# Start addresses modulo 256 of the split-weight rings and the gated sums in a differential-attention and retention trunk

## The chip, the cores and the metric

The kernel runs on one core of a Trainium2 chip. The metric is the time of one execution on the device in microseconds (us), as the median of several runs.

## The reference

Two inputs of 512 rows by 1024 columns (`x_prompt` and `x_sample`) go through the same two layers and a final RMS norm. All is fp32.

```python
for i in range(DEPTH):                       # DEPTH = 2
    h = rms_norm(x, norm_g[i], NORM_EPS)
    if i % 2 == 0:  x = x + diff_attention(h, da_w_in, ..., da_w_out, lambda_init)
    else:           x = x + bidir_retention(h, ret_w_in, ..., ret_w_out)
return rms_norm(x, final_norm_g, NORM_EPS)
```

Differential attention: `proj = h @ w_in` gives q and k (16 heads of 128, with rotary embedding), v and a gate (2048 each). For each of 8 heads two softmaxes are subtracted, `a = p0 - lam * p1`, and `o = a @ v` (256 columns). `o` is RMS-normed, multiplied by `silu(gate)`, and multiplied by `w_out`.

Bidirectional retention: `proj = h @ w_in` gives q and k (8 heads of 128, rotated), v and a gate (2048 each). For each head a forward and a backward sum over the rows with decaying weights are added; the sum is normed, gated and multiplied by `w_out` in the same way.

## The kernel before

**Split operands.** Every large product works on fp32r operands that are split into a high and a low part, and runs three passes (`PASSES`: high by high, high by low, low by high). Each matmul instruction multiplies a stationary operand of 128 by 128, which is loaded into TensorE beforehand, with a moving operand of 512 or 256 columns, and adds to a PSUM bank.

**Projections.** Each layer's input projection is done with a Strassen-like scheme of seven products over the two inputs and two halves of the weights. `make_b` makes the seven split activations (`B11` ... `T4`, four tiles each, high and low in one tile). A `Unit` handles 256 or 512 columns of the weights: `prep` loads, combines and splits weights into tiles of the ring `ws`; `product` multiplies. In a "pair" unit the weights are stationary and 512 columns of an activation move (the matmul at L599); in a "wide" unit, for v, the activation is stationary and 256 columns of weights move (L609). Results go through ACT, DVE and DRAM to the next stage.

**Attention.** For each head, input and block of 128 rows: `scores` (L1116, stationary q, moving k of 512 columns), exponentials on ACT, the difference, transposes (L1161) and `av` (L1181, stationary v, moving `aT` of 256 columns). `weigh` multiplies by the gate and splits the result into `oT` (two tiles, high and low), and `out_step` multiplies it by the output weights (L891: stationary `oT`, moving a `ws` tile of 512 columns) and adds to the rows `x` with the norm's factor. **Retention** has `state2` (L1339), `score2` (L1315) and `av2` (L1359 with stationary v and moving `aT` of 256 columns, L1367), and the same `weigh` and `out_step`.

**Order.** Every operation is entered in a `Plan` with a guessed cost and the buffers that it reads and writes. The plan simulates the engines and issues the instructions in the order that it finds. It knows buffers, not addresses.

**Where the tiles lie.** SBUF is given out by pools in this order: `sm` (small columns, each taking 32 bytes), `cp` (activations that are not in the arena, tables), `ar` (the arena), `wk` (all rings of work tiles: `ws` of 7, `raw`, `st`, `c`, `e`, `m`, `os`). The arena is one tile, cut by hand:

```python
arena = ar.tile([P, 18 * 1024 + 80], F32R, tag="arena", name="arena")
lo = 32 + at * 1024 + shift                  # in floats; slot number at, shift 0, 16 or 32
```

`ssf` holds sums of squares for the input and final norms: twelve columns of one float, each a tile of its own in `sm` (L917, L924, L1017).

In the built program the starts within a partition are these. Sizes of tiles and steps inside them are multiples of 256 bytes, so each start modulo 256 holds for all slices that the matmuls read.

| what | byte | modulo 256 |
|---|---|---|
| `cp` tiles, activations among them | 2,848 and on | 32 |
| arena | 52,896 | 160 |
| slots with shift 0: activations; attention's q, `aT`; retention's v | | 32 |
| slots with shift 16: attention's k, v; retention's q, `aT`, `kt` | | 96 |
| slots with shift 32: `oT`; retention's k | | 160 |
| `wk`: `ws` and all other rings | 126,944 and on | 224 |

Of the kernel before, what the change touches and what calls it, by code (L numbers as in the profile page):

```python
# [9 lines left out]
F32 = mybir.dt.float32  # L10
F32R = mybir.dt.float32r
# [4 lines left out]
P = 128  # L16
S = 512
# [236 lines left out]
def trunk_kernel(  # L254
# [12 lines left out]
    sm = ctx.enter_context(tc.tile_pool(name="sm", bufs=1))  # L267
    cp = ctx.enter_context(tc.tile_pool(name="cp", bufs=1))
    ar = ctx.enter_context(tc.tile_pool(name="ar", bufs=1))
# [7 lines left out]
    places = {}  # L277
    cnt = [0]

    def view(pool, tag, i, size, shape, dt=F32):  # L280


        if size % 16 and pool in (cp, wk):
            pool = sm
        if (tag, i) not in places:
            places[tag, i] = pool.tile([P, size], F32, tag=f"{tag}{i}", name=f"{tag}_{i}", bufs=1)
        n = math.prod(shape[1:])
        t = places[tag, i][0:shape[0], 0:n]
        if dt != F32:
            t = t.bitcast(dt)  # L290
        if len(shape) == 3:
            t = t.rearrange("p (a b) -> p a b", a=shape[1])
        elif len(shape) == 4:
            t = t.rearrange("p (a b c) -> p a b c", a=shape[1], b=shape[2])
        return t

    def work(tag, shape, bufs, dt=F32, name=None):
        size = SIZE.get(tag, shape[1])
        return Buf(plan, tag, bufs, lambda i: view(wk, tag, i, size, shape, dt))

    arena = ar.tile([P, 18 * 1024 + 80], F32R, tag="arena", name="arena")

    def slot(n, shape, dt=F32R, shift=0):

        size = math.prod(shape[1:])
        at = None if n in (12, 13) or n >= 20 else n if n < 12 else n - 2
        if at is None:
            assert not shift  # L310
            cnt[0] += 1
            label = f"b_{cnt[0]}"
            return Buf(plan, f"b{n}", 1, lambda i: cp.tile(shape, dt, tag=f"b{n}", name=label))
        assert dt == F32R
        lo = 32 + at * 1024 + shift

        def make(i):
            t = arena[:, lo:lo + size]
            return t.rearrange("p (a b) -> p a b", a=shape[1]) if len(shape) == 3 else t
        b = Buf(plan, f"b{n}", 1, make)  # L320
        b.also = Buf(plan, f"edge{at + 1 if shift else at}", 1, None)
        return b

    def const(shape, tag, dt=F32, size=None):
        return Buf(plan, tag, 1, lambda i: view(cp, tag, i, size or math.prod(shape[1:]), shape, dt))
# [27 lines left out]
    def bank(tag, name=None):  # L353
        return Buf(plan, tag, BUFS[tag], lambda i: view(pj if tag == "pj" else sc, tag, i, S, [P, S]))
# [469 lines left out]
        return rr  # L824

    def new_oT(g):
        return [slot(16 + 2 * g + a, [P, 2, S], F32R, 32) for a in range(2)]

    def load_qk(src, i, shift):
        t = slot(i, [P, 2, S], F32R, shift)  # L830
# [339 lines left out]
    def av(i):  # L1170

        h, g, t = tiles[i]
        aT, v = st[i]['aT'], vt[h, g]
        o = bank("o")

        def fn():
            n = 0
            for e in range(2):
                for a, b in PASSES:
                    for j in range(NT):  # L1180
                        nc.tensor.matmul(o[:, e * 256:(e + 1) * 256], v[b][:, j, e * P:(e + 1) * P], aT[a][:, j, :],  # L1181
                                         start=(n == 0), stop=(n % 12 == 11), skip_group_check=True)
                        n += 1
        pe(2.76, fn, [*aT, *v], [o])
        if t == 0:
            settle(h - 1, g)
            oT[h, g] = new_oT(g)
        st[i].update(o=o, sq=weigh(o, sg[h, g], oT[h, g], t // 2, GUARD))
# [160 lines left out]
    def av2(b, c):  # L1349
# [29 lines left out]
        if c == 0:  # L1379
            settle(h - 1, g)  # L1380
            oT[h, g] = new_oT(g)
# [152 lines left out]
```

## Time and profile before

| | |
|---|---|
| median of 3 runs | 1808.67 us (1808.62 to 1810.62) |
| profiled execution, span | 1807.0 us from its first to its last instruction |
| profiled execution, own time | not given apart from its span; the runs' median is 1.67 us above the span |
| TensorE matmuls, weight loads | busy 99% and 86% of the span, 10,299 each |
| VectorE (DVE), ScalarE (ACT), GpSimd (POOL) | busy 82%, 50%, 9% |
| granted TensorE clock | 0.999 |

How to read it: the profile lists groups of instructions by line and tiles, with their busy time, the mean duration of one in ns, and the idle time before them. Matmuls are pipelined and their ends are modelled: a matmul of 512 columns is shown with about 390 ns although the next one starts about 230 ns after it. The time from one start to the next is read from stretches of many matmuls. PE stands for the matmuls, PEld for the weight loads, which run beside matmuls.

### The profile page before, as it was taken

To read this page: it belongs to the slowest core of one execution; us is meant where nothing else is said; L and a number is where in the kernel's file an instruction comes from. 1 tells how busy PE (TensorE), PEld (TensorE's weight loads), DVE (VectorE), ACT (ScalarE), POOL (GpSimd) and SP (SyncE) were. 2 spreads that over 40 slices of the span, in tenths; PEclk is the share of its full clock that TensorE was granted. 3 is DMA by queue.
4 is the path that set the end of the run, shared out by engine and by line. 5 is a ranking of instruction groups with operands and counts; after the bars stand their busy time and mean duration, and the time that the engine had idled before them with its cause. 6 is when DMAs were issued, how large, how long until landed. Compare 5 with 4: busy or idle time off the path is not lost.

```text
span 1807.0 us, 27780 instructions
## 1 busy us (share of the span) xinstructions
PE 1794.9 (99%) x10299; PEld 1558.1 (86%) x10299; DVE 1477.1 (82%) x2319; ACT 895.1 (50%) x1856; POOL 169.5 (9%) x323
## 2 busy tenths in 40 slices
PE   9999999999999999999999999999999999999998
PEld 6789889898988888888888888898989898888887
DVE  7958787778699888888888897787887967888887
ACT  7753444433434565554555866444434355444346
POOL 1000000000000022222322300000000000111113
PEclk9999999999999999999999999999999999999999
DMA  6444455555545685444554524464657559765662
GB/s 217 134 126 137 161 140 178 184 168 155 174 126 175 201 334 198 178 156 159 190 204 140 190 73 146 140 210 146 205 156 228 151 170 396 272 238 182 225 218 94
DMA packets 162767, 328.81 MB, mean 182 GB/s; under 512 B 12724, under 2 KB 76872, under 8 KB 162632
## 3 DMA queue, kind: packets, MB, share of 16 engines
q1 hardware_dynamic: 162304, 326.71, 54.1%
q8 instruction: 81, 1.33, 0.3%
q14 instruction: 54, 0.44, 0.1%
q10 hardware_dynamic: 328, 0.34, 0.1%
HBM read 209.55 MB, written 117.44 MB: 181 GB/s over the span
## 4 chain that ended last, share of the span: by engine, by line
PE 93%; DVE 2%; DMA 2%; ACT 2%; issue 1%; POOL 0%; SPq 0%; POOLq 0%; DVEq 0%; ACTq 0%
PE pj L599 20%; PE pj L891 19%; PE sc L599 10%; PE pj L609 10%; PE o L599 8%; PE o L1181 5%; PE sc L1116 5%; PE sc L609 5%; PE o L609 2%; PE o L1359 2%; PE tp L1161 2%; PE sc L1315 1%; PE o L1367 1%; PE tp L1339 1%; DMA raw<-in_ret_w_out_dram 1%
## 5 line engine op out<-in xcount | busy, mean ns | idle before, releaser
L891 PE MATMUL pj<-ws,arena 128*128 128x512 f32 x1542 | 391.2, 397 | 0.0
L891 PEld LDWEIGHTS pj<-ws,arena 128*128 128x128 f32 x1542 | 277.7, 188 | 52.7
L599 PE MATMUL pj<-b,ws 128*128 128x512 f32 x1080 | 265.0, 392 | 0.0
L599 PEld LDWEIGHTS pj<-b,ws 128*128 128x128 f32 x1080 | 201.4, 188 | 43.0
L403 DVE TENSOR_TENSOR ws<-st,ws 128x512 fp32r<-128x512 f32 (+1 forms) x192 | 147.9, 774 | 74.8 <-ACT ws L400 56.7
L896 DVE SCALAR_TENSOR_TENSOR b<-pj,crr,b 128x512 f32<-128x512 f32 (+1 forms) x257 | 189.9, 744 | 21.4 <-PE pj L891 21.0
L403 DVE TENSOR_TENSOR ws<-raw,ws 128x512 fp32r<-128x512 f32 (+1 forms) x164 | 141.5, 868 | 71.3 <-ACT ws L400 61.0
L400 ACT CAST ws<-st 128x512 fp32r<-128x512 f32 (+1 forms) x192 | 132.4, 693 | 121.4 <-PE pj L599 36.4
L599 PE MATMUL sc<-arena,ws 128*128 128x512 f32 x768 | 186.8, 392 | 0.0
L599 PE MATMUL o<-arena,ws 128*128 128x512 f32 x744 | 180.0, 393 | 1.1 <-ACT m L385 0.6
L599 PEld LDWEIGHTS sc<-arena,ws 128*128 128x128 f32 x768 | 144.0, 188 | 31.3
L400 ACT CAST ws<-raw 128x512 fp32r<-128x512 f32 (+1 forms) x164 | 125.7, 772 | 87.0 <-PE o L599 45.0
L599 PEld LDWEIGHTS o<-arena,ws 128*128 128x128 f32 x744 | 138.4, 188 | 31.7 <-DVE arena L463 1.4
L599 PE MATMUL pj<-arena,ws 128*128 128x512 f32 x648 | 160.3, 392 | 0.4 <-DVE arena L463 0.4
L599 PEld LDWEIGHTS pj<-arena,ws 128*128 128x128 f32 x648 | 120.8, 188 | 26.7 <-DVE arena L463 0.7
L1134 ACT ACTIVATE b<-sc,nm 128x512 f32<-128x512 f32 x128 | 88.0, 689 | 66.9 <-DVE nm L1124 66.5
L636 ACT COPY c<-pj 128x512 f32<-128x512 f32 x104 | 60.9, 586 | 119.7 <-PE pj L599 66.4
L609 PE MATMUL pj<-ws,b 128*128 128x256 f32 x960 | 116.8, 276 | 0.0
L609 PEld LDWEIGHTS pj<-ws,b 128*128 128x128 f32 x960 | 113.2, 188 | 0.7
L1116 PE MATMUL sc<-arena 128*128 128x512 f32 x384 | 101.2, 395 | 0.3 <-ACT b L1134 0.3
L1181 PEld LDWEIGHTS o<-arena 128*128 128x128 f32 x768 | 93.1, 188 | 2.7
L1181 PE MATMUL o<-arena 128*128 128x256 f32 x768 | 93.7, 278 | 0.0
(207 smaller groups left out, 2855.9 us busy)
## 6 DMA issues: line engine op xcount, KB each, us to landing
qk<-os SPq DMA_DIRECT2D x192, 256.0 KB, 3.6
arena<-qk SPq DMA_DIRECT2D x96, 512.0 KB, 5.8
raw<-in_da_w_in_dram SPq DMA_DIRECT2D x64, 512.0 KB, 5.1
v<-os SPq DMA_DIRECT2D x64, 512.0 KB, 4.3
arena<-v SPq DMA_DIRECT2D x64, 512.0 KB, 4.1
raw<-in_ret_w_in_dram SPq DMA_DIRECT2D x48, 512.0 KB, 4.8
os<-g SPq DMA_DIRECT2D x32, 512.0 KB, 7.4
g<-e SPq DMA_DIRECT2D x48, 256.0 KB, 4.6
```

The costliest lines, as they stand in the source:

```text
L400: act(n, lambda: nc.scalar.copy(dst(), src()), r, w)
L403: dve(n, lambda: nc.vector.tensor_tensor(dst(), src(), hi().bitcast(F32), op=ALU.subtract), r, w)
L599: nc.tensor.matmul(ps.t, a[u][0]()[:, k, :], bt[k][:, v, :], start=(opens and k == 0 and i == 0), stop=(k == 3 and i == 2), skip_group_che ...
L609: nc.tensor.matmul(ps[:, (t % 2) * 256:(t % 2) * 256 + 256], bt[k][:, v, t * P:(t + 1) * P], a[u][0]()[:, k, :], start=(opens and t % 2 == ...
L636: act(S, lambda c=c, ps=ps: nc.scalar.copy(c.t, ps.t), [ps], [c])
L891: nc.tensor.matmul(ps[:, here], o[a][:, e, t * P:(t + 1) * P], u[b][:, e, here], start=(m == 0), stop=(m == 5))
L896: axpy(n, lambda half=half, here=here, ps=ps: nc.vector.scalar_tensor_tensor(half, ps[:, here], rr[:, t % 2:t % 2 + 1], half, op0=ALU.mult ...
L1116: nc.tensor.matmul(s.t, q[:, a, t * P:(t + 1) * P], k[:, b, :], start=(n == 0), stop=(n == 2))
L1134: act(840, lambda j=j, s=s, m=m: nc.scalar.activation(p[:, j, :], s.t, AF.Exp, bias=m.t, accum_out=sm[:, 2 * j + n:2 * j + n + 1]), [s, m] ...
L1161: nc.tensor.transpose(tp[:, j * P:(j + 1) * P], p[:, 0, j * P:(j + 1) * P], ident.t)
L1181: nc.tensor.matmul(o[:, e * 256:(e + 1) * 256], v[b][:, j, e * P:(e + 1) * P], aT[a][:, j, :], start=(n == 0), stop=(n % 12 == 11), skip_g ...
L1359: nc.tensor.matmul(o[:, e * 256:(e + 1) * 256], v_[v][:, 2 * c + j, e * P:(e + 1) * P], a_[:, u, j * 256:(j + 1) * 256], start=(e == 0 and ...
```

## The change

The arena grows by 16 floats (64 bytes). The twelve tiles of `ssf` become columns of one tile of 32 floats (128 bytes instead of 12 x 32 = 384), which moves everything behind them down by 256 bytes and leaves it where it was modulo 256. `wk` begins 192 bytes lower: `ws` and all other work rings start at 32 modulo 256 instead of 224. `oT` gets shift 64 instead of 32 floats, so it starts at 32 modulo 256 instead of 160. Activations, attention's q, k, v and `aT`, and retention's q, k, v, `kt` and `aT` keep their starts modulo 256. Instructions, their number and their order stay.

```diff
         if size % 16 and pool in (cp, wk):
             pool = sm
+            if tag == "ssf":
+                if tag not in places:
+                    places[tag] = sm.tile([P, 16 + 16], F32, tag=tag, name=tag, bufs=1)
+                return places[tag][:, i:i + 1]
...
-    arena = ar.tile([P, 18 * 1024 + 80], F32R, tag="arena", name="arena")
+    arena = ar.tile([P, 18 * 1024 + 96], F32R, tag="arena", name="arena")
...
     def new_oT(g):
-        return [slot(16 + 2 * g + a, [P, 2, S], F32R, 32) for a in range(2)]
+        return [slot(16 + 2 * g + a, [P, 2, S], F32R, 64) for a in range(2)]
```

## The prediction

> **What bounds the kernel now.** I read the page's busy times and chain first, then the groups by line, then the chain in order of time and the timeline at single matmuls.
>
> ```profile
> PE 1794.9 (99%) x10299; PEld 1558.1 (86%) x10299; DVE 1477.1 (82%) x2319; ACT 895.1 (50%) x1856; POOL 169.5 (9%) x323
> PE 93%; DVE 2%; DMA 2%; ACT 2%; issue 1%; POOL 0%; SPq 0%; POOLq 0%; DVEq 0%; ACTq 0%
> ```
>
> TensorE carries 93% of the chain. A busy PE is not a PE at its peak, so the question is how far apart matmuls start ("spacing"). The chain in order of time gives it for unbroken stretches (start, length, what):
>
> ```profile
> 169.04 5.44 PE sc L609 x48
> 210.01 8.24 PE pj L599 x36
> 853.26 2.83 PE o L1181 x24
> 1783.58 13.76 PE pj L891 x60
> ```
>
> A 512-wide matmul follows the last after 8.24/36 = 228.9 ns in L599 and 13.76/60 = 229.3 ns in L891; a 256-wide one after 113.3 ns in L609 and, in this stretch of L1181, after 117.9. Nothing is waited for inside these stretches, and still the spacing isn't one number. Here is what it can depend on: a weight load runs beside the matmul before its own. The timeline shows it where the moving tile changes from `b` to `arena`:
>
> ```profile
> 212.36 1.79 PEld L599 LDWEIGHTS pj<-arena,ws 128*128 128x128 f32 x8
> 212.59 1.76 PE L599 MATMUL pj<-arena,ws 128*128 128x512 f32 x7
> ```
>
> The first load of the new tile starts at 212.36, its matmul at 212.59, one spacing later. So while one matmul streams its moving rows from SBUF, the stationary rows of the next are read from SBUF too. The change alters where these two streams start relative to each other. I call "distance" the start of the moving operand minus that of the stationary one, modulo 256 bytes. From the addresses given above: L599 moves operands at 32 past weights at 224, distance 64. L891 moves weights at 224 past `oT` at 160, distance 64. L609 moves weights at 224 past operands at 32, distance 192. After the change all three have distance 0.
>
> These are the groups concerned (count, busy us, mean ns of one), and L1359, which is 256 wide like L609 but has distance 64 (moving `aT` at 96, stationary `v` at 32):
>
> ```profile
> L891 PE MATMUL pj<-ws,arena 128*128 128x512 f32 x1530 | 389.8, 398 | 0.0
> L599 PE MATMUL pj<-b,ws 128*128 128x512 f32 x1080 | 265.0, 392 | 0.0
> L599 PE MATMUL sc<-arena,ws 128*128 128x512 f32 x768 | 186.8, 392 | 0.0
> L599 PE MATMUL o<-arena,ws 128*128 128x512 f32 x744 | 180.0, 393 | 1.1 <-ACT m L385 0.6 <-DVE arena L463 0.3
> L599 PE MATMUL pj<-arena,ws 128*128 128x512 f32 x648 | 160.3, 392 | 0.4 <-DVE arena L463 0.4
> L609 PE MATMUL pj<-ws,b 128*128 128x256 f32 x960 | 116.8, 276 | 0.0
> L609 PE MATMUL sc<-ws,arena 128*128 128x256 f32 x768 | 89.6, 276 | 0.0
> L609 PE MATMUL pj<-ws,arena 128*128 128x256 f32 x576 | 73.1, 277 | 0.0
> L609 PE MATMUL o<-ws,arena 128*128 128x256 f32 x384 | 45.0, 277 | 0.0
> L599 PE MATMUL sc<-b,ws 128*128 128x512 f32 x120 | 29.1, 391 | 0.0
> L1359 PE MATMUL o<-arena 128*128 128x256 f32 x384 | 48.9, 276 | 0.0
> ```
>
> L599 has 1080 + 768 + 744 + 648 + 120 = 3,360 matmuls; with L891's 1,530 that is 4,890 of 512 columns. L609 has 960 + 768 + 576 + 384 = 2,688 of 256.
>
> **Part 1: the 512-wide matmuls.** Three successive matmuls of L599 near 210.5 us, one row each, from the groups in a window that holds that one alone:
>
> ```profile
> L599 PE MATMUL pj<-b,ws 128*128 128x512 f32 x1 | 0.4, 388 | 0.0
> L599 PE MATMUL pj<-b,ws 128*128 128x512 f32 x1 | 0.4, 392 | 0.0
> L599 PE MATMUL pj<-b,ws 128*128 128x512 f32 x1 | 0.4, 394 | 0.0
> ```
>
> The durations repeat in this cycle of three: A (388), B (392), C (394). Their mean is 391.3 and the mean spacing of the same stretch 228.9, so I read a spacing as the row's duration less 162.4. The cycle doesn't follow the buffers (in L891 it runs at other places of the six), so it is a matter of timing between the two streams. How they stand at distance 0 the trace shows at a few places only: the last matmul of a group overlaps the first weight load of the next line. The last of L599 before L609 has moving 32 and, beside it, a load from 32: distance 0. So has the last of L891 before L599 (224 and 224). One after A, that is in place B (1170.2 us), one in place C (1178.8), one in place A (1032.1):
>
> ```profile
> L599 PE MATMUL pj<-b,ws 128*128 128x512 f32 x1 | 0.4, 397 | 0.0
> L599 PE MATMUL pj<-b,ws 128*128 128x512 f32 x1 | 0.4, 393 | 0.0
> L891 PE MATMUL pj<-ws,arena 128*128 128x512 f32 x1 | 0.4, 389 | 0.0
> ```
>
> Their mean is 393.0, 1.7 ns over the cycle's: one step costs little on average, though place B pays 5. It also throws the next ones off. The three matmuls behind the event at 1032.1 us, behind one of kind C at 626.2 and behind one of kind B at 638.4 (L599 into L1116, 32 and 32):
>
> ```profile
> L599 PE MATMUL pj<-arena,ws 128*128 128x512 f32 x3 | 0.9, 396 | 0.0
> L1116 PE MATMUL sc<-arena 128*128 128x512 f32 x3 | 0.9, 395 | 0.0
> L1116 PE MATMUL sc<-arena 128*128 128x512 f32 x3 | 0.9, 393 | 0.0
> ```
>
> Their mean is 394.7, 3.4 ns over. No run of matmuls at distance 0 exists in this trace; the two bounds nearest to it are +1.7 (the step itself) and +3.4 (what follows it). After the change each matmul is both, and I take +3.0, nearer the followers. Sum: 4,890 x 3.0 ns = 14.7 us, all on the path, since inside these stretches the chain holds nothing but PE. The farther bounds are A for good, 388, which is -3.3 ns or -16.1 us, and the slowest steady row of a 512-wide stretch (L1116 near 856.7 us, distance 64), 398, which is +6.7 ns or +32.8 us:
>
> ```profile
> L1116 PE MATMUL sc<-arena 128*128 128x512 f32 x2 | 0.6, 398 | 0.0
> ```
>
> The Trainium skill, page "TensorE: Matmul & The Clock Gate", section "Step-by-step: what each phase is for", speaks against any cost: it says that TensorE reads SBUF through two independent ports, one for the streamed operand and one for the weights. By that rule this term would be 0. The 388 to 398 of one shape with nothing waited for show that something more is at work here, whether or not it is the distance.
>
> **Part 2: the 256-wide matmuls.** L609 at distance 192 and L1359 at distance 64 both stand at 276, the 113.3 ns spacing. A step at distance 0 (the last of L1181, moving 32, before L1116's load from 32, at 1002.5 us) gives
>
> ```profile
> L1181 PE MATMUL o<-arena 128*128 128x256 f32 x1 | 0.3, 277 | 0.0
> ```
>
> one ns more. I take 0 for the 2,688. The other end is L1181's 117.9 ns, +4.6 each or +12.4 us; a gain below 113.3 no row shows.
>
> **Part 3: the other rings.** All of `wk` moves from 224 to 32, so `raw`, `st`, `c`, `e`, `m` and `os` do as well. A DVE operation on tiles at 224 and one whose SBUF tiles are in the arena at 32, and the same for ACT:
>
> ```profile
> L403 DVE TENSOR_TENSOR ws<-st,ws 128x512 fp32r<-128x512 f32 x160 | 108.9, 685 | 56.7 <-ACT ws L400 56.2
> L403 DVE TENSOR_TENSOR arena<-tp,arena 128x512 fp32r<-128x512 f32 x64 | 43.8, 685 | 4.9 <-ACT arena L400 4.4
> L400 ACT CAST os<-m 128x512 fp32r<-128x512 f32 x64 | 38.5, 621 | 34.3 <-DVE m L701 33.3 <-DMA qk<-os 0.9
> L400 ACT CAST b<-m 128x512 fp32r<-128x512 f32 x8 | 4.6, 619 | 0.0
> ```
>
> 685 and 685, 621 and 619: the start makes no difference there, and PE's 99% hides a nanosecond or two in either. Transfers are the same in number, size and order; I cost them at nothing, hidden by the buffers that PE works ahead of, and the chain's 2% of DMA (36 us) is what they could touch if they did change.
>
> **Part 4: `ssf` as one tile.** No instruction is added, and the plan orders by buffers, not addresses. If neighbouring columns made one engine wait for another, this row pair shows the place:
>
> ```profile
> L924 POOL TENSOR_TENSOR rsf<-ssf,mhalf x16: 537/554/1304, 1007.1 to 1801.9; 128x1 f32<-128x1 f32 x16
> POOL rsf L924 <- ACT ssf L917: 22.5, 12, 6.5
> ```
>
> Sixteen powers of about 0.55 us on a POOL that is busy 9% of the span; each is needed a norm later. Only the last, at 1801.9, has no cover: below 0.6 us. I take 0.
>
> **Sum.** On the profiled execution, 1807.0 + 14.7 = 1821.7 us of span. The runs' median of 1808.67 lies 1.67 above that span, so 1823.4.
>
> **Rivals.** *Much slower* (0.18): at distance 0 the streams lock in the worst way seen, 398 at 512 columns and 117.9 ns at 256. For it: both are steady states of this trace, and L1181 stays in its one for 24 matmuls. Against it: single steps at distance 0 gave 389, 393 and 277. Price: 32.8 + 12.4 = 45.2 us, 1853.9.
>
> *No difference* (0.13): timing alone makes the cycle, and a constant distance only shifts where it begins. For it: distance 64 and 192 give the same 276, and L1181 shows both 113.3 and 117.9 at one distance. Against it: in place B the same step costs 392 at distance 64 and 397 at 0. Price 0, 1808.7. The skill's two ports, above, would make this the outcome.
>
> *Faster* (0.19): distance 0 keeps the load of the next weights in step with the streaming operand, so that they never want the same rows and every matmul is an A. For it: place A at distance 0 cost 389, hardly over 388, and a 256-wide matmul at 0 is as cheap as any. It decides if the step after an A is an A again. Against it: the step behind 1032.1's 389 was among three that mean 396. Price: -3.3 x 4,890 = -16.1 us, 1792.6.
>
> That the change doesn't do what it says I exclude: 384 bytes less 128 leaves 256, so all before the arena keeps its place modulo 256, and 64 bytes more of arena put `wk` at 32.
>
> **Numbers.** My forecast (0.50) is slower by 8 to 17 us for the bounds 1.7 and 3.4, so 1816 to 1826 of its own. Measurement tells about 0.2%, 3.6 us, from no change. Faster 0.19, same 0.13, slower 0.50 + 0.18 = 0.68. The range has to reach into the two outer rivals: 1797 to 1846 leaves out the last third or so of each of their ways, some 0.15 together.
>
> **What would show it.** Right: L599's stretch of 36 takes about 8.35 us instead of 8.24, its rows mean 394 to 395, L609's stay at 276, and DVE and ACT keep their durations. Wrong: L599 at 388 (faster), at 391 to 392 (no difference), or at 398 with L609 at 281 (much slower). If the time moves while these rows don't, the cause is not the distance but a wait, which the chain would name outside PE.

## The result and the profile after

The changed kernel takes 1823.58 us (median of 4 runs, 1822.9 to 1823.79) against 1808.77 before (1808.62 to 1810.62): a ratio of 1.008, 95% interval 1.0066 to 1.0094. The forecast was 1823.4. The time is the forecast one; the way to it is not. Some executions, of the kernel before too, show a mean granted clock of 0.998 instead of 0.999 and take about 1.8 us more; the text says where a profile is of such an execution. Lines behind 284 stand 4 further down after the change: L599 is L603, L609 is L613, L891 is L895, L1359 is L1363, L1367 is L1371.

The page after, first part and chain:

```profile
span 1821.8 us, 27780 instructions
PE 1808.3 (99%) x10299; PEld 1577.3 (87%) x10299; DVE 1477.6 (81%) x2319; ACT 895.5 (49%) x1856; POOL 169.9 (9%) x323
PE 93%; DVE 2%; DMA 2%; ACT 2%; issue 1%; POOL 0%; SPq 0%; POOLq 0%; DVEq 0%; ACTq 0%
```

TensorE's busy time grew by 13.4 us and that of its weight loads by 19.2; DVE and ACT stayed within 0.5. The chain has the same shares. They are whole percents, 18 us each, and can't exclude a wait alone; but span less TensorE's busy time is 13.5 us after 12.1, so waits grew by 1.4 us net at most. Now the chain in order of time (start, length, what):

```profile
168.91 5.76 PE sc L613 x48
211.36 8.16 PE pj L603 x36
```

The same stretches took 5.44 and 8.24 us before. That is, the 256-wide matmuls of the projections went from 113.3 to 120.0 ns apart, the 512-wide ones from 228.9 to 226.7: one of the two slower, the other faster. The groups by line of the changed kernel (count, busy us, mean ns of one):

```profile
L895 PE MATMUL pj<-ws,arena 128*128 128x512 f32 x1530 | 389.5, 398 | 0.0
L603 PE MATMUL pj<-b,ws 128*128 128x512 f32 x1080 | 263.1, 390 | 0.0
L603 PE MATMUL sc<-arena,ws 128*128 128x512 f32 x768 | 185.2, 390 | 0.0
L603 PE MATMUL o<-arena,ws 128*128 128x512 f32 x744 | 178.8, 391 | 1.1 <-ACT m L389 0.6 <-DVE arena L467 0.3
L603 PE MATMUL pj<-arena,ws 128*128 128x512 f32 x648 | 159.2, 390 | 0.7 <-ACT arena L473 0.4 <-DVE arena L467 0.3
L613 PE MATMUL pj<-ws,b 128*128 128x256 f32 x960 | 123.0, 283 | 0.0
L613 PE MATMUL sc<-ws,arena 128*128 128x256 f32 x768 | 94.8, 283 | 0.0
L613 PE MATMUL pj<-ws,arena 128*128 128x256 f32 x576 | 76.6, 284 | 0.0
L1363 PE MATMUL o<-arena 128*128 128x256 f32 x384 | 50.4, 280 | 0.0
L613 PE MATMUL o<-ws,arena 128*128 128x256 f32 x384 | 47.3, 283 | 0.0
L603 PE MATMUL sc<-b,ws 128*128 128x512 f32 x120 | 28.8, 389 | 0.0
```

L613 sums to 341.7 us, 17.2 more than before. L603 sums to 815.1, 6.1 less. L895 is 0.3 less. L1363, whose own operands kept their starts, is 1.5 more. These four give +12.3 of the 14.8 us. L1116, L1181, L1339 and L1367, short groups of attention and retention that kept their starts too, are 2.5 more together. Idle time adds 1.4 us, and smaller groups give as much back.

### The profile page after: what moved, and what is told of

Same layout as the page of the kernel before. It is cut to its first block, busy times and chain, and to the rows that moved or that the text cites. A ratio compares the mean times of both kernels' runs of the same rounds, so it can differ in the third digit from the quotient of the medians.

```text
span 1821.8 us, 27780 instructions
## 1 busy us (share of the span) xinstructions
PE 1808.3 (99%) x10299; PEld 1577.3 (87%) x10299; DVE 1477.6 (81%) x2319; ACT 895.5 (49%) x1856; POOL 169.9 (9%) x323
## 4 chain that ended last, share of the span: by engine, by line
PE 93%; DVE 2%; DMA 2%; ACT 2%; issue 1%; POOL 0%; SPq 0%; POOLq 0%; DVEq 0%; ACTq 0%
PE pj L603 20%; PE pj L895 18%; PE sc L603 10%; PE pj L613 10%; PE o L603 8%; PE sc L613 5%; PE o L1185 5%; PE sc L1120 5%; PE o L613 3%; PE o L1363 2%; PE tp L1165 2%; PE o L1371 1%; PE tp L1343 1%; PE sc L1319 1%; DMA raw<-in_ret_w_out_dram 1%; DMA raw<-in_da_w_in_dram 1%
## 5 line engine op out<-in xcount | busy, mean ns | idle before, releaser
L895 PE MATMUL pj<-ws,arena 128*128 128x512 f32 x1542 | 390.9, 397 | 0.0
L895 PEld LDWEIGHTS pj<-ws,arena 128*128 128x128 f32 x1542 | 277.6, 188 | 52.8
L603 PE MATMUL pj<-b,ws 128*128 128x512 f32 x1080 | 263.1, 390 | 0.0
L603 PEld LDWEIGHTS pj<-b,ws 128*128 128x128 f32 x1080 | 201.4, 188 | 41.2
L603 PE MATMUL sc<-arena,ws 128*128 128x512 f32 x768 | 185.2, 390 | 0.0
L603 PE MATMUL o<-arena,ws 128*128 128x512 f32 x744 | 178.8, 391 | 1.1 <-ACT m L389 0.6
L603 PEld LDWEIGHTS sc<-arena,ws 128*128 128x128 f32 x768 | 143.9, 188 | 29.8
L603 PEld LDWEIGHTS o<-arena,ws 128*128 128x128 f32 x744 | 138.4, 188 | 30.6 <-DVE arena L467 1.4
L603 PE MATMUL pj<-arena,ws 128*128 128x512 f32 x648 | 159.2, 390 | 0.7 <-ACT arena L473 0.4
L603 PEld LDWEIGHTS pj<-arena,ws 128*128 128x128 f32 x648 | 120.9, 188 | 25.9 <-DVE arena L467 0.6
L613 PE MATMUL pj<-ws,b 128*128 128x256 f32 x960 | 123.0, 283 | 0.0
L613 PEld LDWEIGHTS pj<-ws,b 128*128 128x128 f32 x960 | 119.1, 192 | 0.6
L613 PE MATMUL sc<-ws,arena 128*128 128x256 f32 x768 | 94.8, 283 | 0.0
```

The costliest lines, as they stand in the source:

```text
L603: nc.tensor.matmul(ps.t, a[u][0]()[:, k, :], bt[k][:, v, :], start=(opens and k == 0 and i == 0), stop=(k == 3 and i == 2), skip_group_che ...
L613: nc.tensor.matmul(ps[:, (t % 2) * 256:(t % 2) * 256 + 256], bt[k][:, v, t * P:(t + 1) * P], a[u][0]()[:, k, :], start=(opens and t % 2 == ...
L895: nc.tensor.matmul(ps[:, here], o[a][:, e, t * P:(t + 1) * P], u[b][:, e, here], start=(m == 0), stop=(m == 5))
```

## The experiments

**Theories.** D: the distance between the streaming operand's start and that of the operand being loaded, modulo 256 bytes, sets the spacing of a long run. Rivals: the gated sums carry the loss (O); a wait through the other rings or the `ssf` tile (W); the absolute start of a stream (A).

**One ring at a time, and the starts split by kind of unit.** Four kernels, beside 1808.69 us for the kernel before. The first is the changed kernel with `oT` back at 160:

```diff
-        return [slot(16 + 2 * g + a, [P, 2, S], F32R, 64) for a in range(2)]
+        return [slot(16 + 2 * g + a, [P, 2, S], F32R, 32) for a in range(2)]
```

> The ring of split weights at 32 as in the changed kernel, the gated sums oT back at 160. Theory D (the distance between the streaming and the loaded operand sets the spacing in a long run): L599 and L609 stand as in the changed kernel, 226.7 and 120 ns, which is -6 and +17 us against before; only L891 (distance now 128) and the lines that start behind it can differ: 1820 us, within 3. Rival O (the gated sums carry the loss): 1809. Rival W (a wait from the other rings or the ssf tile, which are here as in the changed kernel): 1823 to 1824, with the added time outside L609.

The second leaves `oT` at 32 and puts `wk` back to 224:

```diff
-    arena = ar.tile([P, 18 * 1024 + 96], F32R, tag="arena", name="arena")
+    arena = ar.tile([P, 18 * 1024 + 144], F32R, tag="arena", name="arena")
```

> The gated sums oT at 32 and ssf as one tile as in the changed kernel, the ring of split weights and all other work rings back at 224. Theory D: L599 and L609 as before the change, 229 and 113.3 ns; L891 at distance 192 and the short groups behind it may move by a few us: 1807 to 1812. Rival O: 1823. Rival W for the ssf tile alone: above 1809 with a longer wait on POOL in the norm of the rows.

The third has both arena and `oT` so that all starts are as before the change, and then shifts the weights of pair units alone:

```diff
+        if tag == "ws" and "ws" not in places:
+            places["ws"] = wk.tile([P, 6 * 1088 + 1040], F32, tag="ws", name="ws", bufs=1)
+        if tag == "ws":
+            lo = 1088 * i + (16 if len(shape) == 4 else 0)
+            t = places["ws"][:, lo:lo + math.prod(shape[1:])].bitcast(dt)
...
-        return work("e", [P, S], 8, name=name)
+        return work("e", [P, S], 7, name=name)
```

> Weights of pair units (stationary in L599) start at 32 and weights of wide units (moving in L609) and of the output product (moving in L891) at 224, by an offset inside the ring's places; oT at 160; one buffer less in ring e, to make room. Theory D: L599 has distance 0 and 226.7 ns, L609 distance 192 and 113.3 ns, L891 as before: 1808.8 - 6 = 1803 us, within 2, plus what the missing e buffer costs (see the run of that alone). Rival O or W (distance is not the cause): 1809 or more.

The fourth is the third without the shift:

> Starts as before the change, all distances as before, ssf as one tile, and one buffer less in ring e: the comparison for the run with split starts. If neither the ssf tile nor the eighth buffer of e matters: 1808.8, within 1. If one of them matters: above 1810, with waits on e or ssf in the chain.

Measured, in this order: 1825.65 us (ratio 1.0095, 1.008 to 1.011), 1815.36 (1.0033, 1.0021 to 1.0044), 1813.55 (1.0026, 1.0016 to 1.0036), 1808.9 (0.9999, 0.999 to 1.0009).

The last settles W for two of its places: `ssf` as one tile and one `e` buffer less cost nothing, so the third can be read against it. In the first, L603 and L613 stand as in the changed kernel (but for 1.4 us in one L603 group, since its profile has a clock of 0.998): the weights' ring alone makes the +17 and the -6. Its time is 2.7 us above D's range all the same. L891, now at distance 128, takes 3.0 us more than before, and L1359 and L1367 take 2.1 more:

```profile
L895 PE MATMUL pj<-ws,arena 128*128 128x512 f32 x1530 | 392.8, 400 | 0.0
```

O in its pure form is out, but the second run is 3 us above what D gave it. About half of that is clock: four of its six executions, the profiled one among them, have 0.998 (0.73 from 25 to 31 us of the span, where the kernel before has 1.00), and the two others took 1813.42 and 1813.8 us. Its groups:

```profile
L895 PE MATMUL pj<-ws,arena 128*128 128x512 f32 x1530 | 393.2, 400 | 0.0
L603 PE MATMUL pj<-b,ws 128*128 128x512 f32 x1080 | 264.9, 392 | 0.0
L613 PE MATMUL sc<-ws,arena 128*128 128x256 f32 x768 | 89.6, 276 | 0.0
L1363 PE MATMUL o<-arena 128*128 128x256 f32 x384 | 50.2, 279 | 0.0
L1371 PE MATMUL o<-arena,b 128*128 128x256 f32 x192 | 27.7, 279 | 0.0
```

L603 and L613 are as before, but for 1.5 us more in the L603 group that runs at the lower clock. L895, of which only the stationary operand moved (distance 64 to 192), has +3.4 us: where the loaded operand lies does slow the streaming one. And L1363 and L1371 have +1.3 and +0.7 although nothing of theirs moved. They run directly or soon behind L895. Before, L1367 (now L1371) had:

```profile
L1367 PE MATMUL o<-arena,b 128*128 128x256 f32 x192 | 27.0, 276 | 0.0
```

The longest stretch of L891, 13.76 us before, gives the spacing at the other three distances: 0 (changed kernel), 128 (first run) and 192 (second run).

```profile
1798.53 13.63 PE pj L895 x60
1802.00 13.97 PE pj L895 x60
1790.00 14.02 PE pj L895 x60
```

That is 227.2, 232.8 and 233.7 ns after 229.3: here too the distance orders the spacings.

The third run missed. The chain of it:

```profile
74.59 8.16 PE pj L611 x36
167.94 5.65 PE sc L621 x48
1172.81 4.10 PE pj L621 x36
```

The 512-wide matmuls are at 226.7 as expected (L599 is L611 here), but the 256-wide ones (L621) hold 117.7 ns at the same distance of 192 at which they hold 113.3 in the kernel before. So D in its simple form falls: one distance, two spacings. This run alone shows both: in each of retention's four wide units an early stretch of 36 has 113.9 ns (third line), and all longer ones have 117.7. What differs from the kernel before is the runs before L621, now at 226.7, and the places of the ring, which are the same modulo 256 but lie elsewhere (in one tile, 1,088 floats apart). From here on theory E: a run has more than one steady spacing, and the entry decides which.

**Other distances, and all starts shifted together.** Four kernels beside 1808.92 us. In the first two only the offset of wide units' weights in the split ring changes, with base and arena so that pair units stay at 32 and the output product at 224. The first has 16 here, the second 32 in its place:

```diff
-            lo = 1088 * i + (16 if len(shape) == 4 else 0)
+            lo = 1088 * i + (0 if len(shape) == 4 else 16 if shape[1] == 4 else 48)
```

> As the first run with split starts (pair units' weights at 32, the output product's at 224, oT at 160, one e buffer less), but the wide units' weights at 96, so L609 has distance 64 instead of 192. Theory E (a run of 256-wide matmuls has more than one steady spacing; which one it falls into depends on distance and on how it is entered): either 113.3 ns, which gives 1803 us, or 117.8, which gives 1813.5; L1359, which had distance 64 before, stood at 113.3 more often than not, so 113.3 is a little likelier. Theory D in its simple form (each distance has one spacing) says 113.3 and 1803, since 64 gave 113.3 in L1359.

> As the run before, but the wide units' weights at 160, so L609 has distance 128. Only single steps of 128 were seen: they cost 117 to 118 ns where the other matmuls around stood at 113. Theories D and E both expect 117.8 or more: 1813 to 1820 us.

The third is the kernel before with `arena` 16 floats larger than in the changed one and `ssf` as one tile:

> All work rings at 96, oT at 160: L599 has distance 192, L609 64, L891 192. Theory D: L599 not at 226.7; single steps of 192 cost 2 to 7 ns more than those of 64 in the same place, so 230 to 233 ns, +3 to +13 us; L609 113.3 to 117.8, 0 to +12 us; L891 as in the run with oT alone moved, +3. Together 1813 to 1835. If distance were without effect: 1809.

The fourth is the kernel before with `ssf` as one tile and a pad of 32 bytes in front. It keeps every distance and moves all by 32 bytes:

```diff
+    pad = sm.tile([P, 8], F32, tag="pad", name="pad", bufs=1)
     ident = const([P, P], "ident")
```

> Every tile of SBUF used by TensorE starts 32 bytes later than before the change (activations at 64, weights at 0, oT at 192, k at 128), all distances as before; ssf as one tile. Theories D and E: the distances decide alone, so 1808.8, within 2, with 228.9 and 113.3 ns. Rival A (the absolute start of a stream decides, for instance against lines of 64 bytes): L599 and L609 leave these spacings, down to 213 and 107 if a stream that starts on a line has one line less to read, which would be about 5% less time.

Measured, in this order: 1814.82 us (1.0033, 1.002 to 1.0046), 1820.5 (1.0063, 1.0048 to 1.0078), 1839.8 (1.017, 1.0153 to 1.0187), 1809.1 (1.0001, 0.9992 to 1.0011). The third missed its range by 4.8 us: L603 takes 14.1 us more where 13 was the upper end, L613 11.2 more, and L1363 and L1371 2.1 more, which the estimate hadn't. The chains of the third (first three lines) and of the fourth:

```profile
75.64 8.40 PE pj L603 x36
171.39 5.65 PE sc L613 x48
1814.56 14.02 PE pj L895 x60
```

```profile
75.20 8.24 PE pj L604 x36
168.97 5.44 PE sc L614 x48
```

Shifted together, the spacings are those of before to the last digit: rival A falls for a shift of 32 bytes. It falls for 128 bytes as well: L895 has distance 192 here with its operands at 96 and 160, and in the run with `oT` alone moved with 224 and 32, and its long stretch takes 14.02 us in both. At distance 192 the 512-wide matmuls take 8.40/36 = 233.3 ns, the worst of the four distances. L621 at distance 64 stood at 117.7 in the first of these runs, at 128 at 120.0 in the second (5.65 and 5.76 us for 48). So 64 gave the slower of E's two values, not the likelier one and not that of D.

**Is it the entry?** The split kernel again (distance 192 in the wide units), where the first matmul of P1, P2 and P4 of each wide unit is cut into narrower ones over the same columns, another cut in each of the eight units. The sums are the same; the two streams are shifted once against each other.

```diff
+    KICKS = [{(0, 0): [0, 128, 256]}, {(0, 0): [0, 64, 256]}, {(0, 0): [0, 192, 256]},
+             {(0, 0): [0, 128, 256], (0, 1): [0, 128, 256]}, {(0, 0): [0, 32, 256]}, {(0, 0): [0, 96, 256]},
+             {(0, 0): [0, 64, 128, 192, 256]}, {(0, 0): [0, 160, 256]}]
...
+                        cuts = KICKS[self.nth_wide].get((k, i), [0, 256]) if t == 0 and op in KICK_OPS else [0, 256]
+                        for c0, c1 in zip(cuts, cuts[1:]):
```

> The split starts with L609 at distance 192, and in each of the eight wide units the first matmul of P1, P2 and P4 is cut into pieces of another width (128+128, 64+192, 192+64, two matmuls of 128+128, 32+224, 96+160, 4x64, 160+96 in turn), which shifts the streams against each other once at the entry of a run. Theory E (two steady spacings at distance 192, chosen at the entry): some cuts send the rest of the run to 113.3 ns, others leave it at 117.8; with all of them at 113.3 the time would be 1805, with none 1816. Rival D2 (with L599 at distance 0 something that lasts makes L609 slower, not its entry): all runs stay at 117.8, 1814 to 1816.

One run: 1814.4 us beside 1808.64 (at a clock of 0.998, which accounts for about 1.8 us of it). The chain in order of time; one stretch of each of the eight units in turn:

```profile
169.84 5.44 PE sc L633 x48
303.92 5.65 PE sc L633 x48
381.55 5.44 PE sc L633 x48
458.71 5.65 PE sc L633 x48
1186.39 5.44 PE sc L633 x48
1284.28 5.65 PE sc L633 x48
1364.30 5.44 PE sc L633 x48
1443.37 5.65 PE sc L633 x48
```

Two values and nothing between: 113.3 ns behind the cuts 128+128, 192+64, 32+224 and 4x64, 117.7 behind the others. The stretches shown lie behind further matmuls of the same unbroken run, so what one cut matmul sets at the entry holds. A cut can also make a run slower: the stretches of 36, at 113.9 ns without cuts, take 4.24 and 4.25 us, 117.9 ns, behind the cuts 96+160 and 160+96. That is E, and D2 falls. Each cut was tried in one unit only, and fast and slow units alternate; but without cuts, and with one cut for all (next), the long runs of all eight units stand alike, so the units themselves don't explain it.

**The best of it, and the same cuts at distance 0.** The cut 128+128 in all units of the split kernel, and the eight cuts in the changed kernel itself, beside 1808.67 us:

> Split starts as in the first run with them, and the first matmul of P1, P2 and P4 of every wide unit cut into 128+128. Theory E: L599 at 226.7 ns, -5 us; L609 at 113.3 ns in all long runs; each of about 28 cuts costs about 0.12 us, +3 us. Together 1806 us, 2 to 3 below the kernel before. If the cut only works in the one unit in which it was tried: 1814.

> The changed kernel itself (all distances 0) with the eight cuts at the entries of L609, one kind for each wide unit. Theory E1 (at distance 0 only one steady spacing exists): all runs of L609 return to 120 ns, whatever the cut, 1824 to 1827 us. Theory E2 (at distance 0 too there is a faster one that is only never entered): some units at 113.3, each of them worth 2 us.

Measured: 1805.2 us (ratio 0.9981, 0.9972 to 0.9989) and 1827.12 (1.0102, 1.0086 to 1.0117). The groups of the first, the chain of the second:

```profile
L618 PE MATMUL pj<-b,ws 128*128 128x512 f32 x1080 | 263.0, 390 | 0.0
L631 PE MATMUL sc<-ws,arena 128*128 128x256 f32 x768 | 89.6, 276 | 0.0
```

```profile
132.17 8.16 PE pj L612 x36
168.83 5.76 PE sc L625 x48
```

The first has both fast spacings and beats the kernel before by 3.5 us (2 to 5 by the interval) and the changed one by 18. The rings behind `ws` (`st`, `c`, `os`, most of `e` and `m`) lie at 32 in it as in the changed kernel, so W has no ground there either. In the second no cut changes the spacing: L625 is back at 120.0 everywhere, E1, and the cuts only add 3.5 us to the changed kernel's time. At distance 0 no other steady spacing was reached by any of the eight cuts.

**The fourth distance.** All rings and `oT` at 160 (`arena` at 128 instead of 96 floats, `oT` shift 32), one run:

> All work rings at 160, oT at 160: L599 and L609 have distance 128, L891 distance 0. It completes the four distances in steps of 64. L609 at 120 ns as in the run with the wide units' weights at 160, +17 us; L599 between 226.7 and 233.4 ns, the ends seen at 0 and 192, -7 to +15 us; L891 as in the changed kernel, 0: 1818 to 1841. If the spacing at 512 columns rose step by step with the distance (226.7, 229, ..., 233.4) it would be 231, and the time 1833.

1837.54 us beside 1808.76. The chain:

```profile
75.41 8.36 PE pj L603 x36
170.97 5.76 PE sc L613 x48
302.98 5.69 PE o L613 x48
1812.41 13.64 PE pj L895 x60
```

It shows 232.2 ns at 512 columns, inside the range given. L613 stands at 120.0 in the first wide unit, and in the long runs of the seven others at about 118.6 (third line): two spacings at this distance too. L895, at distance 0 with both operands at 160, is where it was with both at 32. All distances in steps of 64 bytes:

| distance | 512 columns, ns apart | 256 columns, ns apart |
|---|---|---|
| 0 | 226.7 | 120.0 |
| 64 | 228.9 | 117.7 |
| 128 | 232.2 | 120.0 or 118.6 |
| 192 | 233.3 | 113.3 or 117.7, by the entry |

The table is of the projections' long runs. L1359's shorter ones at distance 64 stood near 113.3 in the kernel before (276 ns in the row), so 64 has more than one spacing as well.

## Why the prediction was right, and where not

**Right in time, wrong in both terms.** It had 14.7 us on the 512-wide matmuls and 0 on the 256-wide ones. The groups show -6.4 (L599 and L891) and +17.2. That the sums agree is chance: two errors of 21 and 17 us cancel, helped by some 4 us in other groups and idle time that the sum didn't hold.

**The step that failed in part 1** is the reading of "+1.7 and +3.4" as bounds for a long run. They were single steps of distance 0 in the midst of others, and what followed them was at distance 64 again, a disturbed cycle. Two of the three rows behind the +3.4 are of L1116 besides, compared with L599's cycle, and L1116's own mean before is 395:

```profile
L1116 PE MATMUL sc<-arena 128*128 128x512 f32 x384 | 101.2, 395 | 0.3 <-ACT b L1134 0.3
```

Left to itself, distance 0 has no cycle: L603 settles at one value, 226.7 ns, 2.2 below the old mean. The rival *Faster* described just this, "every matmul is an A" (A 226, its bound 388 against the 389 and 390 measured), and for the 4,890 it had the direction, with 6.4 us instead of 16.1: L891 is broken up, mostly into runs of 6 and 12, and gained 0.3 us in all.

**The step that failed in part 2** is "I take 0", from one L1181 matmul of 277 ns. The changed kernel shows why one step misleads. Two rows of it, the first matmul of L613 behind L603, at 163.0 us, and the two next:

```profile
L613 PE MATMUL o<-ws,arena 128*128 128x256 f32 x1 | 0.3, 277 | 0.0
L613 PE MATMUL o<-ws,arena 128*128 128x256 f32 x2 | 0.4, 283 | 0.0
```

The first step of a run at distance 0 is as cheap as ever; the next is not, and the run stays at 120.0 ns to its end. The upper end that I gave, 117.9, was too low as well: long runs pay 6.7 ns each, and the groups 17.2 us instead of 12.4.

**The rivals.** *Much slower* had the lock and the place of it (L609) right, and 512 columns wrong. *No difference* is refuted for this kernel: in the run with `oT` alone moved, only the stationary operand of L891 lies elsewhere, and its streaming matmuls take 393.2 us instead of 389.8. The Trainium skill, page "TensorE: Matmul & The Clock Gate", section "Step-by-step: what each phase is for", states two independent read ports. This run doesn't agree with a cost of 0 drawn from that: whatever the ports are, the two reads are not independent in time.

**Parts 3 and 4 held.** The rows of the changed kernel that answer to those of before:

```profile
L407 DVE TENSOR_TENSOR ws<-st,ws 128x512 fp32r<-128x512 f32 x160 | 109.0, 686 | 55.3 <-ACT ws L404 55.0
L404 ACT CAST b<-m 128x512 fp32r<-128x512 f32 x8 | 4.6, 619 | 0.0
POOL rsf L928 <- ACT ssf L921: 22.5, 12, 6.4
```

686 after 685, 619 after 619, and the wait on `ssf` is 22.5 us in all as before.

**A term that was missing:** lines that moved nothing. L1359 and L1367 pay +1.5 and +0.7 us, and nearly the same in the run where only `oT` moved. The runs together tie this to L891, behind which they start: L1359 takes 48.8 to 48.9 us in every kernel in which L891 has distance 64, the split ones too, and 50.2 to 50.4 in every one in which it has another. No run changed the entry of these lines by itself, so that they keep the spacing with which they are entered stays likely, not shown.

**Open.** What in SBUF or TensorE makes the two reads meet, and why some cuts of the entry lead to the faster spacing and others don't. Distances between the steps of 64 bytes were not run.

## What to carry to other kernels

Where TensorE is the bound, read matmul spacing from stretches of the chain, not from busy shares, and look whether the same shape has several; if so, the relative start of streaming and stationary tiles is a thing to set, for each shape by itself (here 0 for 512 columns, 192 for 256). A steady run can't be priced from single steps: equal matmuls can settle at more than one spacing, and cutting a matmul at the entry can be worth it (here 24 cuts, three in each of eight units, took the split kernel from 1813.55 to 1805.2 us). A total that comes out right proves none of its terms: compare them group by group.

## What the runs showed of the hardware that was not expected

The spacing of equal fp32r matmuls depends on the distance between the streamed operand and the one that is loaded beside it, by up to 6.6 ns of 230 and 6.7 of 113, and a common shift by 32 bytes changes nothing (1809.1 against 1808.92 us). All rings at the worst place tried cost 1.7% (1839.8 us). At distance 192, 256-wide matmuls have two steady spacings, 113.3 and 117.7 ns, which hold over runs of 240 matmuls and are chosen by how the run begins.
